# A mixture-of-experts layer: GpSimd's computing behind the routing moved to VectorE and ScalarE

## The chip, the cores and the metric

The kernel runs on one core of a Trainium2 chip (trn2). The metric is the device time of one execution in microseconds, as the median of several runs. The engines are named as in the profile: PE is TensorE's matmuls, PEld its weight loads, DVE is VectorE, ACT is ScalarE, POOL is GpSimd, SP is SyncE, whose queue issues most transfers. Matmuls run at one of two clock levels, 1.2 or 2.4 GHz; the profile gives the granted clock as a share of the higher.

## What is computed

One transformer layer on 512 tokens of width 2048, in float32: a projection, three mixers (spatial gating, a chunked recurrence, latent attention), an output projection, a layer norm, a router that picks two of 32 experts for each token, the experts, and a last layer norm. The change touches what comes behind the router:

```python
def hierarchical_moe(x, ...):
    # group_prob, top 1 group; in it the top 2 experts; gates = g_val * softmax(e_val)
    ...
    def run_block(args):
        xb, e = args
        h = jax.nn.silu(xb @ w_gate[e]) * (xb @ w_up[e])
        return h @ w_down[e]
    ys = lax.map(run_block, (xs, blk_exp)).reshape(P, D)
    out = jnp.zeros((N + 1, D), x.dtype).at[slot_tok].add(ys * slot_gate[:, None])
    return out[:N].reshape(B, S, D)
...
ffn = hierarchical_moe(x, ...)
x = layer_norm(DEEPNORM_ALPHA * x + ffn, ln2_g, ln2_b)
```

## The kernel before, in words

The program is written out by hand for each engine: every engine runs its instructions in the order in which the Python code issues them, and waits on semaphores where one needs another's result. Tokens lie in four blocks of 128 (`NB`), the width in 16 pieces of 128 (`KD`). `z[b]` holds a block's residual, later its result.

**Weights.** `Ring` streams weight chunks of 128x1024 float32 (512 KB) in the order of use. SP loads a chunk into a raw buffer (line 81); ACT copies its high part in float32r (line 96), DVE subtracts to get the low part (line 97), into one of four pairs of buffers (three in `whl`, one in an X slot). PE multiplies by both parts. `done` gives a pair back and `pump` issues the next copy, subtraction and load. The second and fourth quarter of each down projection (`WHOLE`) use the raw chunk as it is, without a split.

**Experts.** For each of the 32 experts `gather` zeroes one of two row buffers (`xgs`, slots M0 and B3, 128x2048; line 1202 for the first two, line 1328 for the others) and fetches the tokens' rows by an indirect transfer of POOL (line 1323), so many as the expert has, in eight sizes. `rows` turns them on PE (1348), applies ln1's gain on ACT and DVE (1437, 1364) and splits them (161, 162). `up` runs 16 chunks: four matmuls each (1390, 1391) if the expert has at most 64 rows, six (156 to 158) if more. `down` of the expert before runs behind it: four quarters of two chunks, each evicted with the gate as scale on ACT (1430), then `scatter` adds the rows to `yd` in DRAM by indirect transfers of POOL (1338). In the loop, pass e begins with `gather(e + 2)`, then comes `up(e)`, with the row work of expert e + 1 hooked between the chunks, then `down(e - 1)`. Behind pass 12 and pass 29 SP loads a layer norm's gain and bias, broadcast to 128 partitions (line 1554).

**Gates.** `gates` (1282 to 1296) turns the tokens' gates into a table by expert: a product and a subtraction on POOL (1283, 1287), a copy on ACT between them (1286), eight matmuls (1291), two steps on DVE. It is hooked into `up(0)`, the matmuls stand ahead of its last chunk.

**Tail.** Behind the last scatter the halves of `yd` are loaded back in 512 KB pieces (line 1578, `H` is the two halves of the width, `yd[i]` half i of all tokens), seven by SP and one by POOL. Each block is then: addition to `z` with the sum taken along (`add`, 1629), mean, squares on ACT (1638), root on ACT (1591, 1592) with a refinement on DVE (1597 to 1605), and the normalization in two passes (`norm`, 1610; `scale_dve`, 1617) with a store for each piece. POOL and ACT take block 3's additions (1632, 1635) and the normalization of block 1 and a quarter of block 3 (1622, 1626).

## Time and profile before

| | us |
|---|---|
| median of 3 runs | 1947.78 |
| lowest, highest | 1945.18, 1947.96 |
| the profiled execution, its own time | 1946.49 |
| span of its trace | 1944.7 |
| busy in it: PE, DVE, ACT, POOL | 1818.7, 1422.1, 1260.5, 277.1 |

The span runs from the first to the last instruction of the trace, 1.8 us under the time of the same execution. Times in the rows count from the span's start. The routing ends near 760, the experts run from there to about 1890, the tail follows. An engine's busy time is an average over all of these, so each is read by itself. In the rows "idle before" is how long the engine stood still ahead of the row, and behind the arrow is what ended that wait; the releaser is inferred. A row of the windows view gives a stretch and its length, then busy time and count of PE, PEld, DVE, ACT and POOL, the granted clock, the DMA share and GB/s.

### The profile page before, as it was taken

To read this page: it belongs to the slowest core of one execution; us is meant where nothing else is said; L and a number is where in the kernel's file an instruction comes from. 1 tells how busy PE (TensorE), PEld (TensorE's weight loads), DVE (VectorE), ACT (ScalarE), POOL (GpSimd) and SP (SyncE) were. 2 spreads that over 40 slices of the span, in tenths; PEclk is the share of its full clock that TensorE was granted. 3 is DMA by queue.
4 is the path that set the end of the run, shared out by engine and by line. 5 is a ranking of instruction groups with operands and counts; after the bars stand their busy time and mean duration, and the time that the engine had idled before them with its cause. 6 is when DMAs were issued, how large, how long until landed. Compare 5 with 4: busy or idle time off the path is not lost.

```text
span 1944.7 us, 25279 instructions
## 1 busy us (share of the span) xinstructions
PE 1818.7 (94%) x8235; PEld 1370.1 (70%) x8236; DVE 1422.1 (73%) x2031; ACT 1260.5 (65%) x1763; POOL 277.1 (14%) x200
## 2 busy tenths in 40 slices
PE   9999999999999996899999999999999999999980
PEld 7888888887787895666666666666766666667640
DVE  5656433566564456888989888898898989898757
ACT  4533363635452224788878888887888878788753
POOL 1000000020000001212121121212112121121114
PEclk9999999999999997899999999999999999999995
DMA  7222223223154225799999999999999999999983
GB/s 250 97 87 76 76 76 98 87 87 130 44 209 155 91 83 202 264 361 383 388 385 384 389 337 399 396 379 390 375 373 398 389 382 389 381 372 391 331 284 137
DMA packets 139942, 510.72 MB, mean 263 GB/s; under 512 B 17664, under 2 KB 17712, under 8 KB 137200
## 3 DMA queue, kind: packets, MB, share of 16 engines
q1 hardware_dynamic: 130608, 476.64, 65.2%
q0 software_dynamic: 8576, 30.26, 6.0%
q8 instruction: 93, 1.52, 0.3%
q10 hardware_dynamic: 576, 1.57, 0.2%
q14 instruction: 89, 0.73, 0.1%
HBM read 488.53 MB, written 22.02 MB: 263 GB/s over the span
## 4 chain that ended last, share of the span: by engine, by line
issue 50%; PE 36%; POOL 6%; DVE 4%; DMA 2%; POOLq 1%; ACT 0%; another core or an unknown queue 0%; SPq 0%; ACTq 0%; DVEq 0%
PE acc L156 10%; PE acc L157 10%; PE acc L158 10%; POOL yd L1338 2%; POOL B L1328 2%; POOL M L1328 1%; DMA yd<-M,idx 1%; POOLq L1309 1%; PE aux L495 1%; PE acc L860 1%; DMA B<-x1d,idx 1%; DVE B L1617 0%; PE acc L861 0%; POOLq L1315 0%; PE aux L831 0%
## 5 line engine op out<-in xcount | busy, mean ns | idle before, releaser
L97 DVE TENSOR_TENSOR whl<-X,whl 128x1024 fp32r<-128x1024 f32 x312 | 377.4, 1221 | 100.0 <-ACT whl L96 68.5
L97 DVE TENSOR_TENSOR whl<-wraw,whl 128x1024 fp32r<-128x1024 f32 (+1 forms) x222 | 269.6, 1217 | 227.6 <-ACT whl L96 210.1
L96 ACT ACTIVATE whl<-wraw 128x1024 fp32r<-128x1024 f32 (+1 forms) x222 | 235.2, 1063 | 220.7 <-PE acc L157 94.7
L96 ACT ACTIVATE whl<-X 128x1024 fp32r<-128x1024 f32 x312 | 330.8, 1074 | 60.9 <-PE acc L158 40.3
L1391 PE MATMUL acc<-whl,B 128*128 128x512 f32 x696 | 288.2, 414 | 15.6 <-DVE whl L97 15.6
L1390 PE MATMUL acc<-whl,B 128*128 128x512 f32 x696 | 295.0, 424 | 1.4 <-ACT whl L96 0.7
L1338 POOL DMA_INDIRECT yd<-M,idx x64 | 89.5, 1399 | 870.3 <-ACT M L1430 870.3
L1391 PEld LDWEIGHTS acc<-whl,B 128*128 128x128 f32 x696 | 132.0, 190 | 86.8 <-DVE whl L97 59.5
L158 PE MATMUL acc<-whl,B 128*128 128x512 f32 (+1 forms) x480 | 181.3, 378 | 0.0
L157 PE MATMUL acc<-whl,B 128*128 128x512 f32 (+1 forms) x424 | 166.0, 391 | 14.6 <-DVE whl L97 14.5
L156 PE MATMUL acc<-whl,B 128*128 128x512 f32 (+1 forms) x424 | 179.2, 423 | 0.0
L1390 PEld LDWEIGHTS acc<-whl,B 128*128 128x128 f32 x696 | 132.0, 190 | 31.8 <-issue 4.3
L156 PE MATMUL acc<-X,whl 128*128 128x512 f32 x384 | 151.1, 394 | 0.1
L157 PE MATMUL acc<-X,whl 128*128 128x512 f32 x384 | 149.7, 390 | 0.2 <-DVE X L162 0.2
L158 PE MATMUL acc<-X,whl 128*128 128x512 f32 x384 | 149.6, 390 | 0.0
L1426 PE MATMUL acc<-X,X 128*128 128x512 f32 x308 | 141.2, 592 | 0.0
L97 DVE TENSOR_TENSOR X<-X,X 128x1024 fp32r<-128x1024 f32 x105 | 128.0, 1219 | 17.5 <-ACT X L96 13.2
L96 ACT ACTIVATE X<-X 128x1024 fp32r<-128x1024 f32 x105 | 112.6, 1073 | 20.4 <-PE acc L158 15.0
L1430 ACT ACTIVATE M<-acc,X 128x512 f32<-128x512 f32 x128 | 87.4, 683 | 50.8 <-PE acc L1426 44.2
L157 PEld LDWEIGHTS acc<-whl,B 128*128 128x128 f32 x424 | 80.5, 190 | 47.7 <-DVE whl L97 27.0
L1391 PE MATMUL acc<-X,B 128*128 128x512 f32 x232 | 98.0, 422 | 9.4 <-DVE X L97 9.4
L158 PEld LDWEIGHTS acc<-whl,B 128*128 128x128 f32 x480 | 91.0, 190 | 15.7
(461 smaller groups left out, 3660.4 us busy)
## 6 DMA issues: line engine op xcount, KB each, us to landing
X<-w_down SPq DMA_DIRECT2D x169, 512.0 KB
X<-w_gate SPq DMA_DIRECT2D x160, 512.0 KB
X<-w_up SPq DMA_DIRECT2D x160, 512.0 KB
wraw<-w_gate SPq DMA_DIRECT2D x69, 512.0 KB
wraw<-w_up SPq DMA_DIRECT2D x69, 512.0 KB
wraw<-w_in SPq DMA_DIRECT2D x64, 512.0 KB
wraw<-w_down SPq DMA_DIRECT2D x64, 512.0 KB
B<-w_up SPq DMA_DIRECT2D x27, 512.0 KB
```

Of the source, the lines that this page charges most:

```text
L96: nc.scalar.activation(h[:, s], r[:, s], AF.Copy)
L97: nc.vector.tensor_tensor(l[:, s], r[:, s], h[:, s].bitcast(F32), op=OP.subtract)
L156: mm(o, a[0], b[0], start=start, stop=False)
L157: mm(o, a[0], b[1], start=False, stop=False)
L158: mm(o, a[1], b[0], start=False, stop=stop)
L495: mm(ov[r, j], fl(D)[:, c * P:c * P + r.stop], Dv[:, c, :, 1, :], start=True, stop=True)
L1328: nc.gpsimd.memset(xgs[e % 2], 0.0)
L1338: nc.gpsimd.indirect_dma_start(out=yd[i][:], out_offset=off(index), in_=y[:, H[i]], in_offset=None, bounds_check=T - 1, oob_is_err=False, ...
L1390: mm(o, x, wk[0], start=k == 0, stop=False)
L1391: mm(o, x, wk[1], start=False, stop=k == KD - 1)
L1426: mm(o, hfs[e % 2][:, k * P:(k + 1) * P], w[:, cs], start=k == 0, stop=k == 3)
L1430: act(yts[-1][:, n * 512:(n + 1) * 512], o, AF.Copy, scale=gt[:, EX[e]:EX[e] + 1])
```

## The change

Nothing but indirect transfers stays on POOL behind the routing. (1) `clear` zeroes a row buffer on ACT, as a copy of the constant `one_c`, broadcast over 2048 columns, with scale 0. It replaces the memsets; the first two stand behind `exps`, where the memsets stood ahead of the last block's routing. (2) The product and the subtraction of `gates` go to DVE. (3) The loads of the tail all go through SP, first half of all blocks first. (4) The tail's additions, normalizations and refinements run on DVE, block by block; ACT keeps the squares and the root; `add_pool`, `total`, `norm_act` and `gain` are gone. The last block's second pass goes in four quarters, the others' in halves.

```diff
--- before.py
+++ after.py
@@ -1198,8 +1198,9 @@
     ring.add([r1[:, 0, :]], once=True)
     ring.pump()
     xgs = [slot(t, [DM]) for t in ("M0", "B3")]
-    for t in xgs:
-        nc.gpsimd.memset(t, 0.0)
+
+    def clear(t):
+        act(t, one_c.to_broadcast([P, DM]), AF.Copy, scale=0.0)
 
 
     SIZES = (16, 24, 32, 40, 48, 64, 80, P)
@@ -1257,6 +1258,8 @@
 
     weave(rt_, ranks())
     exps()
+    for t in xgs:
+        clear(t)
     tt(oa[:, L], oh4[:, 0, L], oh4[:, 1, L], op=OP.add)
     mm(o3[:, 0:NE], afterr, oa[:, L], start=False, stop=True)
     mm(oc[:, 0:NE], onesr, oa[:, L], start=False, stop=True)
@@ -1280,11 +1283,11 @@
     gt = carve(NE)
 
     def gates():
-        nc.gpsimd.tensor_tensor(gv, oh, wide(gate, [2 * NB, NE], 2), op=OP.mult)
+        tt(gv, oh, wide(gate, [2 * NB, NE], 2), op=OP.mult)
         hl = tp[:, 0:512].rearrange("p (i a e) -> p i a e", a=2, e=NE)
         yield
         act(hl[:, :, 0], gv, AF.Copy)
-        nc.gpsimd.tensor_tensor(hl[:, :, 1], gv, hl[:, :, 0].bitcast(F32), op=OP.subtract)
+        tt(hl[:, :, 1], gv, hl[:, :, 0].bitcast(F32), op=OP.subtract)
         yield
         o = aux()
         for i in range(2 * NB):
@@ -1325,7 +1328,7 @@
                                          bounds_check=T - 1, oob_is_err=False)
         if e:
             if e > 1:
-                nc.gpsimd.memset(xgs[e % 2], 0.0)
+                clear(xgs[e % 2])
             sized(e, move)
         else:
 
@@ -1573,9 +1576,9 @@
 
     Q = [slice(i * 512, (i + 1) * 512) for i in range(4)]
     ys = [[slot(t, [DM]) for t in ts] for ts in (("M0", "B3"), ("B4", "X1"), ("B7", "X2"), ("X6", "X3"))]
-
-    for i, b in ((0, 0), (0, 1), (0, 2), (1, 0), (1, 1), (0, 3), (1, 2), (1, 3)):
-        (nc.gpsimd if (i, b) == (0, 2) else nc.sync).dma_start(ys[b][1][:, H[i]], yd[i][b * P:(b + 1) * P])
+    for i in range(2):
+        for b in range(NB):
+            nc.sync.dma_start(ys[b][1][:, H[i]], yd[i][b * P:(b + 1) * P])
     sums = carve(NB, 12)
     nc.scalar.preload_act_table_set("natural_log_exp_and_others")
 
@@ -1609,91 +1612,46 @@
         for s in parts:
             stt(ys[b][1][:, s], z[b][:, s], col(b, 8), lng2[:, s], op0=OP.add, op1=OP.mult)
 
-    def store(b, s):
-        nc.sync.dma_start(out[b][:, s], z[b][:, s])
-
-    def scale_dve(b, parts):
+    def scale(b, parts=H):
         for s in parts:
             stt(z[b][:, s], ys[b][1][:, s], rs[:, b:b + 1], lnb2[:, s], op0=OP.mult, op1=OP.add)
-            store(b, s)
-
-    def norm_act(b, parts):
-        for s in parts:
-            act(z[b][:, s], z[b][:, s], AF.Identity, scale=rs[:, b:b + 1], bias=col(b, 7))
-
-    def gain(b, s):
-        for t, op in zip((lng2, lnb2), (OP.mult, OP.add)):
-            nc.gpsimd.tensor_tensor(z[b][:, s], z[b][:, s], t[:, s], op=op)
-
-    def add(b, s, i):
+            nc.sync.dma_start(out[b][:, s], z[b][:, s])
+
+    def add(b, i):
+        s = H[i]
         stt(z[b][:, s], z[b][:, s], 1.0, ys[b][1][:, s], op0=OP.mult, op1=OP.add, accum_out=col(b, i))
 
-    def add_pool(b, s):
-        nc.gpsimd.tensor_tensor(z[b][:, s], z[b][:, s], ys[b][1][:, s], op=OP.add)
-
-    def total(b, s, i):
-        act(ys[b][0][:, s], z[b][:, s], AF.Copy, accum_out=col(b, i))
-
-    def squares(b):
+    def stats(b):
+        add(b, 1)
+        ts(col(b, 8), col(b, 0), col(b, 1), -1.0 / DM, op0=OP.add, op1=OP.mult)
         act(ys[b][0], z[b], AF.Square, bias=col(b, 8), accum_out=col(b, 9))
 
-    def run(*seq):
-
-        for f in seq:
-            if callable(f):
-                f()
-            else:
-                next(f, None)
-
-    for b in range(3):
-        add(b, H[0], 0)
-    add(0, H[1], 1)
-    mean(0)
-    squares(0)
-    root(0)
+        r = rs[:, b:b + 1]
+        act(r, col(b, 9), AF.Ln, scale=1.0 / DM, bias=eps2_c)
+        act(r, r, AF.Exp, scale=-0.5)
+
+    def refine(b):
+
+        r, v, t = rs[:, b:b + 1], col(b, 10), col(b, 11)
+        ts(v, col(b, 9), 1.0 / DM, EPS2, op0=OP.mult, op1=OP.add)
+        stt(t, r, v, r, op0=OP.mult, op1=OP.mult)
+        ts(t, t, -0.5, 1.5, op0=OP.mult, op1=OP.add)
+        tt(r, r, t, op=OP.mult)
+
+    for b in range(NB):
+        add(b, 0)
+    stats(0)
     norm(0, H[:1])
-    add(1, H[1], 1)
-    mean(1)
-    squares(1)
-    root(1)
-    add_pool(3, H[0])
-    total(3, H[0], 0)
-    add_pool(3, H[1])
-    f = refine(0)
-    run(f, lambda: norm(0, H[1:]), f, f, f)
-    scale_dve(0, H[:1])
-    for _ in refine(1):
-        pass
-    norm_act(1, H[:1])
-    gain(1, H[0])
-    add(2, H[1], 1)
-    mean(2)
-    squares(2)
-    root(2)
-    total(3, H[1], 1)
-    norm_act(1, H[1:])
-    gain(1, H[1])
-    scale_dve(0, H[1:])
-    norm(2, H[:1])
-    f = refine(2)
-    run(f, f, f, f)
-    scale_dve(2, H[:1])
-    mean(3)
-    squares(3)
-    root(3)
-    store(1, H[0])
-    norm(2, H[1:])
-    scale_dve(2, H[1:])
-    norm(3, H[:1])
-    f = refine(3)
-    run(f, f, f, f, f)
-    scale_dve(3, H[:1])
-    store(1, H[1])
-    norm_act(3, Q[3:])
-    gain(3, Q[3])
-    norm(3, Q[2:3])
-    scale_dve(3, Q[2:3])
-    store(3, Q[3])
+    stats(1)
+    norm(0, H[1:])
+    stats(2)
+    refine(0)
+    scale(0)
+    stats(3)
+    for b in range(1, NB):
+        norm(b)
+        refine(b)
+        scale(b, Q if b == NB - 1 else H)
 
 
 # ---- launch: one core; the host only lays the inputs out
```

Lines of the new kernel lie three higher from `clear` on: 1430 there is 1433, 1437 is 1440.

On ACT, where one expert's down projection ends and the next pass begins: the eviction of the fourth quarter, then the weight copy of the new pass and the gain step on the rows. Before:

```order
L1430 ACTIVATE M_118_6828<-acc,X_101_3986 128x512
L1315 UNCONDITIONAL_BRANCH
L1384 UNCONDITIONAL_BRANCH
L96 ACTIVATE whl<-wraw 128x1024
L1315 UNCONDITIONAL_BRANCH
L1437 ACTIVATE B_109_5391<-aux,X_101_3986 128x128
```

And now:

```order
L1433 ACTIVATE M_118_6828<-acc,X_101_3986 128x512
L1203 ACTIVATE M_108_5390<-one_c 128x2048
L1318 UNCONDITIONAL_BRANCH
L1387 UNCONDITIONAL_BRANCH
L96 ACTIVATE whl<-wraw 128x1024
L1318 UNCONDITIONAL_BRANCH
L1387 UNCONDITIONAL_BRANCH
L1440 ACTIVATE B_109_5391<-aux,X_101_3986 128x128 x2
```

The clear of a row buffer (`M_108`, slot M0; the next one takes `B_109`, slot B3) stands between the eviction and the copy that follows it.

On DVE in `up(0)`, around the last chunks, weight splits (97) and row splits (162). Before, the gates' steps stood on POOL and not here:

```order
L162 TENSOR_TENSOR B_115_6113<-B_109_5391,B_115_6113 128x512
L97 TENSOR_TENSOR whl<-X_105_5381,whl 128x1024
L1384 UNCONDITIONAL_BRANCH
L97 TENSOR_TENSOR whl<-X_105_5381,whl 128x1024
L162 TENSOR_TENSOR B_115_6113<-B_109_5391,B_115_6113 128x512
L1384 UNCONDITIONAL_BRANCH
L97 TENSOR_TENSOR whl<-B_106_5382,whl 128x1024
L97 TENSOR_TENSOR X_96_3981<-M_107_5383,X_96_3981 128x1024
```

And now:

```order
L162 TENSOR_TENSOR B_115_6113<-B_109_5391,B_115_6113 128x512
L97 TENSOR_TENSOR whl<-X_105_5381,whl 128x1024
L1387 UNCONDITIONAL_BRANCH
L97 TENSOR_TENSOR whl<-X_105_5381,whl 128x1024
L1387 UNCONDITIONAL_BRANCH
L162 TENSOR_TENSOR B_115_6113<-B_109_5391,B_115_6113 128x512
L97 TENSOR_TENSOR whl<-B_106_5382,whl 128x1024
L1290 TENSOR_TENSOR X_110_5395<-X_101_3986,X_110_5395 128x8x32
L97 TENSOR_TENSOR X_96_3981<-M_107_5383,X_96_3981 128x1024
```

The gates' subtraction (1290), which waits for ACT's copy, now has its place between two weight splits.

On SP, the loads of the tail; `yd_2918` and `yd_2919` are the two halves of the sums, and B_125, X_127, X_129, X_131 are blocks 0 to 3. Before:

```order
L1578 DMA B_125_20168<-yd_2918 128x1024
L1578 DMA X_127_20170<-yd_2918 128x1024
L1315 UNCONDITIONAL_BRANCH
L1578 DMA B_125_20168<-yd_2919 128x1024
L1578 DMA X_127_20170<-yd_2919 128x1024
L1578 DMA X_131_20174<-yd_2918 128x1024
L1578 DMA X_129_20172<-yd_2919 128x1024
L1578 DMA X_131_20174<-yd_2919 128x1024
```

And now:

```order
L1581 DMA B_125_20168<-yd_2918 128x1024
L1581 DMA X_127_20170<-yd_2918 128x1024
L1318 UNCONDITIONAL_BRANCH
L1581 DMA X_129_20172<-yd_2918 128x1024
L1581 DMA X_131_20174<-yd_2918 128x1024
L1581 DMA B_125_20168<-yd_2919 128x1024
L1581 DMA X_127_20170<-yd_2919 128x1024
L1581 DMA X_129_20172<-yd_2919 128x1024
L1581 DMA X_131_20174<-yd_2919 128x1024
```

Block 2's first half comes from POOL's queue to this one, and it and block 3's stand ahead of all second halves.

## Rows read from the trace of the kernel before

**Rows 1.** windows view: busy us (count) of five engines, PEclk, DMA, GB/s

```profile
1087.00:1105.00 18.00, 17.11 (x78) 12.08 (x76) 18.00 (x23) 18.00 (x27) 3.49 (x3) 1.00 1.03 384
```

**Rows 2.** timeline of ACT: start, us, line, operation, [idle before <-releaser]

```profile
1078.96 0.63 ACT L161 ACTIVATE B<-X 128x512 fp32r<-128x512 f32 x1 [2.99 <-DVE X L1407]
...
1084.83 0.69 ACT L1430 ACTIVATE M<-acc,X 128x512 f32<-128x512 f32 x1 [1.80 <-PE acc L1426]
...
1085.80 1.06 ACT L96 ACTIVATE whl<-wraw 128x1024 fp32r<-128x1024 f32 x1 [0.28 <-PE acc L1391]
```

**Rows 3.** timeline of DVE at the same change, first weight split

```profile
1086.89 1.22 DVE L97 TENSOR_TENSOR whl<-wraw,whl 128x1024 fp32r<-128x1024 f32 x1 [2.34 <-issue]
```

**Rows 4.** timeline of PE, last chunks of one expert, first of the next

```profile
1071.50 0.51 PE L157 MATMUL acc<-whl,B 128*128 128x512 f32 x1 [0.53 <-DVE whl L97]
...
1085.33 0.39 PE L1391 MATMUL acc<-whl,B 128*128 128x512 f32 x1
```

**Rows 5.** timeline of POOL over the experts: clears, one scatter

```profile
848.28 2.32 POOL L1328 MEMSET M<- 128x2048 f32 x1
...
1222.89 2.29 POOL L1328 MEMSET B<- 128x2048 f32 x1
...
1257.02 2.33 POOL L1328 MEMSET M<- 128x2048 f32 x1
...
1359.30 2.32 POOL L1328 MEMSET B<- 128x2048 f32 x1
...
1397.47 2.34 POOL L1328 MEMSET M<- 128x2048 f32 x1
...
1772.13 2.29 POOL L1328 MEMSET B<- 128x2048 f32 x1
...
1809.59 1.38 POOL L1338 DMA_INDIRECT yd<-M,idx  x1 [4.76 <-ACT M L1430]
```

**Rows 6.** timeline of SP at the first of two added loads

```profile
1212.07 0.42 SPq L1554 DMA_DIRECT2D X<-ln_g  x1
```

**Rows 7.** DMA view: issue, count, KB each of one added load

```profile
X<-ln_g SPq DMA_DIRECT2D x1, 1024.0 KB
```

**Rows 8.** timeline of POOL, PE and ACT in the first two experts

```profile
784.07 1.81 POOL L1328 MEMSET M<- 128x2048 f32 x1 [19.47 <-DVE B L162]
...
797.28 4.85 POOL L1287 TENSOR_TENSOR X<-X,X 128x256 fp32r<-128x256 f32 x1 [7.52 <-ACT X L1286]
...
766.74 2.79 PE L1348 MATMUL aux<-identr,M 128*128 128x128 f32 x12 [7.41 <-DMA M<-x1d,idx]
...
802.18 1.92 PE L1291 MATMUL aux<-X 128*128 128x64 f32 x8 [5.36 <-POOL X L1287]
...
782.73 1.06 ACT L96 ACTIVATE whl<-X 128x1024 fp32r<-128x1024 f32 x1 [0.57 <-PE acc L1391]
```

**Rows 9.** timeline of SP and POOL, loads ahead of the tail

```profile
1887.57 0.33 SPq L1578 DMA_DIRECT2D B<-yd  x1
...
1893.61 0.32 SPq L1578 DMA_DIRECT2D B<-yd  x1
...
1891.32 1.09 POOL L1578 DMA_DIRECT2D X<-yd  x1
```

**Rows 10.** timeline of DVE and ACT in the tail

```profile
1891.02 1.23 DVE L1629 SCALAR_TENSOR_TENSOR B<-B,B 128x1024 f32<-128x1024 f32 x1 [11.77 <-DMA B<-yd]
...
1899.20 1.22 DVE L1629 SCALAR_TENSOR_TENSOR B<-B,B 128x1024 f32<-128x1024 f32 x1 [2.18 <-DMA B<-yd]
...
1900.72 1.28 DVE L1610 SCALAR_TENSOR_TENSOR B<-B,X,X 128x1024 f32<-128x1024 f32 x1
...
1901.92 3.40 DVE L1629 SCALAR_TENSOR_TENSOR B<-B,X 128x1024 f32<-128x1024 f32 x1
...
1932.98 1.63 DVE L1617 SCALAR_TENSOR_TENSOR B<-X,X,B 128x512 f32<-128x512 f32 x1
...
1900.77 2.00 ACT L1638 ACTIVATE M<-B,X 128x2048 f32<-128x2048 f32 x1 [9.30 <-DVE X L1586]
```

## Prediction

> **What bounds the kernel now.** I read the kernel by stretches, since the change touches four of them: the end of the routing, the first two experts, the 28 experts in the steady loop, and the tail. In the loop GpSimd is nearly idle, so what matters is not what leaves GpSimd but what arrives on ScalarE, VectorE and the queues there.
>
> The clears of the loop mark its period: in the timeline of POOL they start at 848.28, 1222.89, 1257.02, 1359.30 and so on [rows 5]. From 848.28 to 1359.30 are 15 periods of 34.07 us; from 1397.47 to 1772.13 are 11 of 34.06. Two periods are longer: 1359.30 to 1397.47 (38.2), and the last one, which I read at the scatter at 1809.59.
>
> One period is a closed loop through three engines, read from who waits for whom. After the last matmul of an expert's first weight chunk (PE, 1085.33 to 1085.72 [rows 4]) ScalarE starts the copy that refills the pair of buffers this chunk freed, at 1085.80 [rows 2], and the row names PE as the releaser. VectorE takes the low part at 1086.89, after 2.34 idle [rows 3]. From there VectorE is never idle: 18.00 of 18.00 us busy from 1087 to 1105, and ScalarE, which feeds it, as full [rows 1]. PE keeps waiting for it (0.53 at 1071.50, one period earlier [rows 4]) until the last down-projection chunks, and from there PE runs unbroken to the next expert's first chunk, 1071.50 to 1085.72. So VectorE's run, about 14 us of PE and one short hop over ScalarE add up to 34.06. Anything put into that hop lengthens the period.
>
> The transfers look as full as VectorE (DMA share 1.03 in the same window [rows 1]), and would be the other candidate for the bound. What speaks against them: at 1212 the kernel loads two extra tensors, of 1024 KB [rows 6, 7], about 5 us of traffic at 384 GB/s, and the periods around it are 34.1 (1222.89 to 1257.02) like all others [rows 5].
>
> **Part 1, clears in the loop.** Each POOL memset of 128x2048 (2.3 us [rows 5]) goes, and one ScalarE copy of 128x2048 comes, right behind the eviction of the last down-projection quarter and ahead of the copy at 1085.80, as the order of ScalarE shows. ScalarE has no such instruction in the trace. A copy of 128x512 lasts 0.63, one of 128x1024 1.06 [rows 2], so 128x2048 lasts about 1.06 + 2 x 0.42 = 1.90; the Square of that shape lasts 2.00 [rows 10]. Neighbours overlap by about 0.1 (eviction at 1084.83 with 0.69, next possible start about 1085.41), so the clear holds ScalarE 1.79. It would start at 1085.41 and let the copy go at 1087.20 instead of 1085.80: **+1.40 us in the hop**. It waits for nothing else: the last reader of the buffer, the row split on VectorE, is done before the down projection. Queued behind it are the weight copies, the two gain steps on the rows, and through them VectorE and PE. ScalarE's own idle ahead of 1085.80 (0.28 in the row) is what it can hide in, and that is already counted. The bounds of one: 1.75 held (+1.36) and 2.00 with no overlap (+1.61).
>
> (The Trainium skill, "ScalarE: Activation LUTs", section "What ACT_TABLE_LOAD costs", gives an activation with immediate scale and bias 186 ns plus 0.833 ns per element, less some 93 ns overlap: an estimate of 1.80 held, and +36.7 us in all by the count below, where the rows give 36.4; no row of before has the operation itself.)
>
> There are 28 such clears. In the two long periods the expert has more than 64 rows, takes six matmuls for each chunk instead of four, and PE sets the pace; there the clear hides. 26 x 1.40 = **+36.4** (35.4 to 41.9). What POOL's memset gives back by leaving: nothing. The memset of that expert starts near 848.28 + 7 x 34.07 = 1086.8, so VectorE's split at 1086.89 runs beside it, and at 1.23 it is as short as an addition of that shape in the tail before POOL computes (1.23 at 1891.02 [rows 10]). The gather that follows starts no later, and its rows are needed one period later.
>
> **Part 2, the first two experts and the gates.** The two clears after the routing hold ScalarE some 3.6 us ahead of three weight copies; PE then stands for 7.41 until the first gathered rows arrive at 766.74 [rows 8], and wants the copies only after those rows are turned and split: nothing. The clear for the third expert waited 19.47 on POOL for VectorE until 784.07, now ScalarE waits there, with its copy of 782.73 behind it [rows 8]: that goes at about 784.0 + 1.8 = 785.8, 3.1 late, and VectorE after it by as much. Against this, PE waited 5.36 for POOL's gate subtraction of 4.85 us (797.28 to 802.13) before 802.18 [rows 8]. On VectorE it costs at most a 128x1024 pass of 1.23 [rows 3]. But it stands there behind the splits, which the clear has made some 3 late, so it ends at about 801 to 801.5: 0.5 to 1 gained, up to 3 if part of the delay is caught up. The fourth clear waits for VectorE in the same way, in an expert that PE paces: 0 to 2 lost. Sum **0** (-3 to +3).
>
> **Part 3, the tail.** Two things. First, the loads: yd's half for block 2 came through POOL at 1891.32, behind the last scatter; now it and block 3's go on SP right behind the first at 1887.57. The load of the second half, at 1893.61, took until 1899.20, 5.6 us, the first one 3.45 (1887.57 to 1891.02) [rows 9, 10]; the difference is the POOL load in its way. Without it 1897.4: 1.8 gained; none if the earlier loads hold up the scatter instead, and 1 lost if they do so by more.
>
> Second, VectorE from there to its end (1899.20 to 1932.98 + 1.63 = 1934.61, 35.4 us). It has passes of 1.2 that last 3.40 (1901.92, where POOL adds at the same time), and a last half pass of 1.63 [rows 10]. These stretches go; the work that POOL and ScalarE did comes to VectorE. Counted anew by undisturbed spacings (addition and mean 1.52, 1899.20 to 1900.72; a pass 1.20, 1900.72 to 1901.92; small steps 0.25, by the 0.3 of that mean): 4 x 1.52 + 14 x 1.20 (8 norms, 6 scales) + 4 quarter scales x 0.65 + 4 x 4 x 0.25 = 6.1 + 16.8 + 2.6 + 4.0 = 29.5. So 5.9 gained. ScalarE's squares (2.00 [rows 10]) end before VectorE asks for them. After its end both kernels have a 256 KB store to finish. Sum 5.9 + 1.8 = **-7.7** (-4.9 to -9.5, the latter with small steps of 0.15).
>
> **Sum.** 36.4 + 0 - 7.7 = +28.7. On the profiled 1946.49: 1975.2; that execution lies 1.3 under the median, so **1976**. By the bounds: 35.4 - 3 - 9.5 = +22.9 to 41.9 + 3 - 4.9 = +40.0, which is 1971 to 1988.
>
> **Rivals.** (a) *The transfers set the period.* Then the 1.40 is absorbed, since ScalarE only waits less for data, and the rest remains: 1947.8 - 7.7 = 1940, faster. For it: the share of 1.03. Against it: the extra loads that cost nothing, and a releaser on PE at the decisive copy. It decides if the 13.1 MB of a period (384 GB/s x 34.06) can't come faster than they do. (b) *The loop gives some back.* VectorE stands idle for 2.34 and more in each period [rows 3]; if work that is now behind the run can move up into that stretch, so that half of 1.40 vanishes, the loop costs 18 and the time is 1947.8 + 18 - 7.7 = 1958. Against it: VectorE takes its work in a fixed order, and its run has no gap to shorten [rows 1]. (c) *PE's clock.* The granted clock is 1.00 in the loop [rows 1]. VectorE's later start puts up to 1.4 more waiting on PE early in each expert; if the clock fell from 2.4 to 1.2 GHz there, matmuls would last twice as long, and PE, which is 95% busy (17.11 of 18.00 [rows 1]), would lose by estimate some 4 us in each period: 26 x 4 on top, about 2080. (The Trainium skill, "TensorE: Matmul & The Clock Gate", Part 1, says that the clock follows how busy PE has been; by that rule a thinner loop is at risk; the trace has no loop as thin.) Against it: PE already waits in the loop (0.53 at 1071.50 [rows 4]) and the clock holds.
>
> **How the numbers follow.** Forecast 0.80, (a) 0.08, (b) 0.09, (c) 0.03. The range reaches over the forecast's bounds and (b): 1957 to 1988. About 0.2% (3.9 us) is what a measurement of this kernel can tell from no change. Faster is (a): 0.08; the same, a mix of (a) and (b), 0.03; slower 0.89.
>
> **What would show it.** The starts of the indirect gathers should lie 35.4 to 35.5 apart, two of them 38.2; VectorE's idle ahead of its first split in each expert should grow from 2.34 to about 3.7, with the same 18 us run behind. In the tail no pass of 1024 columns on VectorE should last over 1.3, and its end should come about 36 us after the first addition, where it was 43.6 (1891.02 to 1934.61). The prediction is wrong if the gathers stay 34.06 apart, or if ScalarE's clear is much off 1.9.

## The result

The changed kernel takes 1973.42 us (median of 4 runs, 1972.23 to 1981.21) where the kernel before takes 1947.72: 25.7 us more. The ratio of the two is 1.0145, with a 95% interval of 1.013 to 1.016. The forecast was 1976, in a range of 1957 to 1988. The profiled execution took 1972.23, with a span of 1970.3, 25.6 over the span of before, and this difference can be split by landmarks that both traces have. The landmarks are the starts of POOL's indirect transfers, VectorE's first addition and its end in the tail.

| us | before | after | difference | forecast |
|---|---|---|---|---|
| start to the scatter of the first expert (its second half) | 847.37 | 848.50 | +1.13 | 0 |
| 28 experts of the loop, to the scatter of expert 28 | 962.22 | 998.34 | +36.12 | +36.4 |
| from there to the last scatter | 80.85 | 82.17 | +1.32 | 0 |
| last scatter to VectorE's first addition | 0.58 | 0.61 | 0 | 0 |
| first addition to the first of the second half | 8.18 | 7.67 | -0.5 | -1.8 |
| from there to VectorE's end | 35.41 | 28.75 | -6.7 | -5.9 |
| VectorE's end to the end of the span | 10.09 | 4.26 | -5.8 | 0 |

Four views of the changed kernel's loop answer to [rows 1 to 4]. The windows view of 18 us behind VectorE's first split of an expert (columns as in [rows 1]):

```profile
1064.50:1082.50 18.00, 16.58 (x72) 11.36 (x72) 18.00 (x24) 18.00 (x26) 0.00 (x0) 1.00 1.02 367
```

The timelines of ACT, DVE and PE at the same change of expert:

```profile
1060.13 0.69 ACT L1433 ACTIVATE M<-acc,X 128x512 f32<-128x512 f32 x1 [1.80 <-PE acc L1429]
1060.72 1.90 ACT L1203 ACTIVATE M<-one_c 128x2048 f32<-128x2048 f32 x1
1062.52 1.04 ACT L96 ACTIVATE whl<-B 128x1024 fp32r<-128x1024 f32 x1
```

```profile
1063.60 1.23 DVE L97 TENSOR_TENSOR whl<-B,whl 128x1024 fp32r<-128x1024 f32 x1 [3.75 <-ACT whl L96]
```

```profile
1060.63 0.39 PE L1394 MATMUL acc<-whl,B 128*128 128x512 f32 x1
```

The row of PE is the last of the four matmuls of the first chunk, as in [rows 4]. It is done at 1061.02, but the copy that this releases starts at 1062.52, 1.50 later instead of 0.08 (1085.72 to 1085.80), since the clear (1.90, start to next start 1.80) stands between it and the eviction. VectorE's idle time grows from 2.34 [rows 3] to 3.75, its releaser is now the copy, and behind it VectorE is busy for 18.00 of 18.00 as before. The DMA share reads 1.02 at 367 GB/s, where [rows 1] has 1.03 at 384.

POOL's timeline in the changed kernel: gathers, which now mark the period, and the scatters that bound the table's stages.

```profile
848.50 1.39 POOL L1341 DMA_INDIRECT yd<-M,idx  x1 [4.73 <-ACT M L1433]
850.29 1.01 POOL L1326 DMA_INDIRECT M<-x1d,idx  x1 [0.40 <-ACT M L1203]
...
1382.02 0.97 POOL L1326 DMA_INDIRECT B<-x1d,idx  x1 [0.43 <-ACT B L1203]
...
1420.41 0.95 POOL L1326 DMA_INDIRECT M<-x1d,idx  x1 [0.52 <-ACT M L1203]
...
1810.29 0.96 POOL L1326 DMA_INDIRECT B<-x1d,idx  x1 [0.46 <-ACT B L1203]
...
1846.84 1.37 POOL L1341 DMA_INDIRECT yd<-M,idx  x1 [4.78 <-ACT M L1433]
...
1929.01 1.32 POOL L1341 DMA_INDIRECT yd<-M,idx  x1 [4.85 <-ACT M L1433]
```

From 850.29 to 1382.02 are 15 periods of 35.45, from 1420.41 to 1810.29 are 11 of 35.44; the one between them is 38.39. Against [rows 5] that is +1.39 in each of 26 periods, and nothing in the two that PE paces (38.32 and 38.35 from scatter to scatter, 38.33 and 38.34 before).

The tail on DVE (timeline), which answers to [rows 10]:

```profile
1929.62 1.22 DVE L1622 SCALAR_TENSOR_TENSOR B<-B,B 128x1024 f32<-128x1024 f32 x1 [11.89 <-DMA B<-yd]
...
1937.29 1.23 DVE L1622 SCALAR_TENSOR_TENSOR B<-B,B 128x1024 f32<-128x1024 f32 x1 [2.23 <-DMA B<-yd]
...
1940.01 1.22 DVE L1622 SCALAR_TENSOR_TENSOR B<-B,X 128x1024 f32<-128x1024 f32 x1
...
1963.30 2.74 DVE L1617 SCALAR_TENSOR_TENSOR B<-X,X,B 128x512 f32<-128x512 f32 x4
```

The addition that lasted 3.40 beside POOL [rows 10] now lasts 1.22, and VectorE ends at 1966.04. What follows differs most. In before, POOL computed almost as long as VectorE (its last row on the timeline of POOL):

```profile
1932.47 1.59 POOL L1626 TENSOR_TENSOR B<-B,B 128x512 f32<-128x512 f32 x1
```

The windows view of the last stretches of before, then of after (last columns: clock, DMA share, GB/s):

```profile
1936.00:1937.00 1.00, 0.00 (x0) 0.00 (x0) 0.00 (x0) 0.00 (x0) 0.00 (x0) 0.50 0.94 322
1937.00:1938.00 1.00, 0.00 (x0) 0.00 (x0) 0.00 (x0) 0.00 (x0) 0.00 (x0) 0.50 0.02 2
1938.00:1944.70 6.70, 0.00 (x0) 0.00 (x0) 0.00 (x0) 0.00 (x0) 0.00 (x0) 0.50 0.00 0
```

```profile
1967.00:1968.00 1.00, 0.00 (x0) 0.00 (x0) 0.00 (x0) 0.00 (x0) 0.00 (x0) 0.50 0.90 305
1968.00:1969.00 1.00, 0.00 (x0) 0.00 (x0) 0.00 (x0) 0.00 (x0) 0.00 (x0) 0.50 0.07 27
1969.00:1970.30 1.30, 0.00 (x0) 0.00 (x0) 0.00 (x0) 0.00 (x0) 0.00 (x0) 0.50 0.00 0
```

Before, no engine and no transfer does anything for the last 6.7 us; after, that is less than 2.

### The profile page after: what moved, and what is told of

It is laid out like the page before. It is cut to its first block, busy times and chain, and to the rows that moved or that the text cites. A ratio compares the mean times of both kernels' runs of the same rounds, so it can differ in the third digit from the quotient of the medians.

```text
span 1970.3 us, 25238 instructions
## 1 busy us (share of the span) xinstructions
PE 1834.7 (93%) x8235; PEld 1370.8 (70%) x8236; DVE 1413.5 (72%) x2041; ACT 1307.5 (66%) x1788; POOL 157.2 (8%) x157
## 4 chain that ended last, share of the span: by engine, by line
issue 50%; DMA 6%; DVE 2%; POOL 1%; POOLq 1%; ACT 0%; PE 0%; DVEq 0%; ACTq 0%
DMA yd<-M,idx 5%; POOL yd L1341 1%; DVE B L1617 0%; POOLq L1312 0%; DVE X L1613 0%; DVE whl L97 0%; DVE B L1622 0%; DMA X<-w_up 0%; POOLq L1318 0%; ACT whl L96 0%; DMA B<-w_down 0%; DMA B<-yd 0%; POOLq L1341 0%; DVE B L1613 0%; DVE X L97 0%
## 5 line engine op out<-in xcount | busy, mean ns | idle before, releaser
L157 PEld LDWEIGHTS acc<-whl,B 128*128 128x128 f32 x424 | 80.5, 190 | 47.6 <-DVE whl L97 27.0
```

Source lines behind the costliest of these rows:

```text
L157: mm(o, a[0], b[1], start=False, stop=False)
```

## The experiments

The table gives each run's stages as above: S the scatter of the first expert, L the 28 experts of the loop, R from there to the last scatter, T from the last scatter to the end of the span, and E the part of T behind VectorE's end. They are read from the profiled execution. The times are medians, those of half_clear, loads_alone, pool_at_end, gates_alone and first_clears of one execution; the kernel before took 1945.8 to 1946.2 in these comparisons.

| | time | S | L | R | T | E |
|---|---|---|---|---|---|---|
| before | 1947.7 | 847.4 | 962.2 | 80.9 | 54.3 | 10.1 |
| after | 1973.4 | 848.5 | 998.3 | 82.2 | 41.3 | 4.3 |
| clears_alone | 1990.8 | 853.9 | 998.3 | 80.4 | 53.7 | 10.1 |
| pool_clears | 1931.0 | 843.0 | 962.1 | 80.8 | 42.2 | 4.3 |
| clear_earlier | 1943.3 | 850.9 | 967.4 | 80.7 | 42.2 | 4.3 |
| clear_in_idle | 1936.5 | 852.1 | 961.9 | 81.1 | 42.3 | 4.2 |
| half_clear | 1944.2 | 844.0 | 976.3 | 80.4 | 41.7 | 4.3 |
| tail_alone | 1935.4 | 848.0 | 961.8 | 82.7 | 41.8 | 4.2 |
| loads_alone | 1946.1 | 847.4 | 962.0 | 82.8 | 52.2 | 10.0 |
| last_quarter | 1939.7 | 846.3 | 962.0 | 81.8 | 47.6 | 4.1 |
| pool_at_end | 1942.0 | 848.8 | 962.0 | 82.6 | 46.9 | 8.7 |
| gates_alone | 1943.1 | 843.9 | 962.4 | 81.6 | 53.4 | 10.1 |
| first_clears | 1945.0 | 846.3 | 962.3 | 80.9 | 53.8 | 10.1 |
| idle_pool23 | 1930.3 | 842.8 | 962.1 | 81.9 | 42.3 | 4.2 |

### The clears in the loop

**clears_alone**: before, with only this line changed (and `clear` defined).

```
-                nc.gpsimd.memset(xgs[e % 2], 0.0)
+                clear(xgs[e % 2])
```

> The kernel before, with only the 30 clears of gather(2) to gather(31) moved from POOL to ACT, in the place that the change gives them; first clears, gates and tail stay as before. Theory (the clear stands in the hop between PE's first chunk and DVE's first split): 26 periods of 35.45 instead of 34.06 (+36.1), +1.3 in the last pass as in the changed kernel, and up to +3 in the second expert, where ACT's copy for the gates now runs late and POOL's subtraction of 4.85 still follows it: 1985 to 1988. Rival (the clears hide and the 26 us come from another part of the change): within 3 us of 1947.7.

Measured: 1990.77, ratio 1.0234 (1.021 to 1.0258), L = 998.34, the same as in the changed kernel. The whole of the loop's loss is this one line. The early part lost 6.5 us, more than the 3 expected: PE's wait for POOL's subtraction is still there, and now comes later (timeline of PE; 802.18 with 5.36 in [rows 8]).

```profile
806.33 1.91 PE L1294 MATMUL aux<-X 128*128 128x64 f32 x8 [5.37 <-POOL X L1290]
```

**pool_clears**: the changed kernel with that line as before, the opposite edit.

```
-                clear(xgs[e % 2])
+                nc.gpsimd.memset(xgs[e % 2], 0.0)
```

> The changed kernel, with only the 30 clears of gather(2) to gather(31) back on POOL; first clears on ACT, gates on DVE and the new tail stay. Theory: periods of 34.06 again, so 1973.4 - 36.1 - 1.3 = 1936, and 1 to 3 less where the third expert's clear no longer holds up ACT: 1933 to 1936. Rival (part of the tail's 13 us hangs on POOL computing nothing at all behind the routing, not on what it does in the tail): the last store's end lies 7 to 8 us ahead of the span's end again, and the time is 1939 to 1942.

Measured: 1930.95, ratio 0.9929 (0.9912 to 0.9946), L = 962.10, E = 4.27. All else in the change is, taken together, a gain, and this kernel beats both of the others. It came out below the expected 1933, since the clears for the third and fourth expert weigh more than I took (below).

**clear_earlier**: the same number of clears on ACT, moved ahead by one eviction.

```
-            if e > 1:
+            if e in (2, 3):
                 clear(xgs[e % 2])
...
+            if n == 2 and e + 4 < NE:
+                clear(xgs[e % 2])
```

> The changed kernel with the clears of gather(4) to gather(31) on ACT as well, but one weight copy earlier: behind the copy that follows the third eviction of the down projection, ahead of the fourth eviction, where ACT stands idle for 1.80 us in each expert. The same instructions on the same engine. Theory (only the hop counts): the clear of 1.79 fits into the idle time, the periods are 34.06 to 34.2, and the time is 1973.4 - 36.1 - 1.3 = 1936, up to 1940. Rival (ACT is full, so 1.8 us more on it cost 1.4 wherever they stand): periods of 35.4, 1970 to 1975.

Measured: 1943.31, ratio 0.9992 (0.9982 to 1.0002). The idea that ACT's total work sets the pace falls: 28 clears on ACT, and 31 of the 36 us are gone. But not all, and the time lies over the expected 1940. The first eleven periods are 34.02 to 34.09; later, where VectorE also applies a layer norm, they are 34.45 to 34.50, two of them 34.9. ACT's timeline in an early and in a late expert:

```profile
1052.35 1.90 ACT L1203 ACTIVATE M<-one_c 128x2048 f32<-128x2048 f32 x1
1054.26 0.69 ACT L1433 ACTIVATE M<-acc,X 128x512 f32<-128x512 f32 x1
1055.23 1.06 ACT L96 ACTIVATE whl<-B 128x1024 fp32r<-128x1024 f32 x1 [0.28 <-PE acc L1394]
...
1502.31 1.91 ACT L1203 ACTIVATE B<-one_c 128x2048 f32<-128x2048 f32 x1
1504.11 0.68 ACT L1433 ACTIVATE M<-acc,X 128x512 f32<-128x512 f32 x1
1504.68 1.06 ACT L96 ACTIVATE whl<-X 128x1024 fp32r<-128x1024 f32 x1
```

In the early expert the copy waits for PE again, by the same 0.28 as in [rows 2]; in the late one it follows the eviction without a wait, so the clear has pushed both. The idle time of that place is smaller there, as ACT's timeline of pool_clears shows at the same point:

```profile
1488.91 0.63 ACT L161 ACTIVATE B<-X 128x512 fp32r<-128x512 f32 x1 [4.28 <-DVE X L1410]
...
1493.49 0.69 ACT L1433 ACTIVATE M<-acc,X 128x512 f32<-128x512 f32 x1 [0.90 <-PE acc L1429]
```

0.90 ahead of the fourth eviction instead of 1.80, and 4.28 three instructions earlier, where VectorE applies the layer norm's gain and bias.

**clear_in_idle**: the clear goes there.

```
-            if n == 2 and e + 4 < NE:
+            if n == 0 and e + 4 < NE:
```

> As clear_earlier, but the 28 clears stand behind the weight copy that follows the first eviction of the down projection. There ACT waits 2.99 us for VectorE's fold of the partial sums in the first experts and 4.3 us from expert 13 on, where VectorE also applies a layer norm's gain and bias; ahead of the fourth eviction it waits 1.80 in the first and only 0.90 in the others. Theory (a clear costs what it exceeds the idle time of its place by, as far as the first split of the next expert waits for it): clear_earlier had periods of 34.05 up to expert 12 and of 34.47 from 13 on; here all normal periods are 34.05, and the time is 1943.3 less 14 x 0.42 = 1937. Rival (the 0.42 come from ACT's total work in the richer periods): they stay at 34.47, 1943.

Measured: 1936.49, ratio 0.995 (0.9936 to 0.9965), L = 961.91, all normal periods 34.01 to 34.09. ACT's timeline shows what is left of the idle time in an early and a late expert:

```profile
1046.65 1.91 ACT L1203 ACTIVATE M<-one_c 128x2048 f32<-128x2048 f32 x1
1049.51 0.63 ACT L161 ACTIVATE B<-X 128x512 fp32r<-128x512 f32 x1 [0.96 <-DVE X L1410]
...
1493.54 1.91 ACT L1203 ACTIVATE B<-one_c 128x2048 f32<-128x2048 f32 x1
1497.73 0.63 ACT L161 ACTIVATE B<-X 128x512 fp32r<-128x512 f32 x1 [2.29 <-DVE X L1410]
```

0.96 and 2.29: a clear of 1.9 costs nothing here. The same instruction costs 36 us, 5 us or nothing by its place alone.

**half_clear**: the clear of the hop, cut in two.

```
-                clear(xgs[e % 2])
+                act(xgs[e % 2][:, H[0]], one_c.to_broadcast([P, DM // 2]), AF.Copy, scale=0.0)
+                nc.gpsimd.memset(xgs[e % 2][:, H[1]], 0.0)
```

> The changed kernel with each of the 30 clears of gather(2) to gather(31) cut in two: 1024 columns on ACT in the hop, the other 1024 on POOL. Theory (the hop takes what exceeds the 0.39 of slack there): a 128x1024 copy holds ACT for 0.95, so periods of 34.06 + 0.56 = 34.6 and 1952. Rival (the cost goes by the work on ACT): half of 1.39, periods of 34.75, 1955. Rival (POOL's memset beside DVE's first splits costs too): over 34.8.

Measured: normal periods of 34.56 to 34.65, mean about 34.60. That is the theory's 34.6 and not 34.75, so the hop absorbs a fixed part of what is put into it and passes on the rest. POOL's half beside VectorE's splits costs nothing. The time (1944.2) lies under the expected 1952 mostly because the early part gained 4.5 us, which I had not counted.

### The first two experts

**gates_alone**: before, with the two steps of `gates` on VectorE.

```
-        nc.gpsimd.tensor_tensor(gv, oh, wide(gate, [2 * NB, NE], 2), op=OP.mult)
+        tt(gv, oh, wide(gate, [2 * NB, NE], 2), op=OP.mult)
...
-        nc.gpsimd.tensor_tensor(hl[:, :, 1], gv, hl[:, :, 0].bitcast(F32), op=OP.subtract)
+        tt(hl[:, :, 1], gv, hl[:, :, 0].bitcast(F32), op=OP.subtract)
```

> The kernel before, with only the gates' product and subtraction on VectorE. Theory (PE's wait for the subtraction was POOL's 4.85 us): PE's wait ahead of the gates' matmuls falls from 5.36 to some 2.2, the value of the changed kernel, and the scatter of the first expert's second half comes at 844 to 845 instead of 846.3 to 848.0 (four executions with before's code up to there); time about 3 less, 1943 to 1945. Rival (the subtraction waits behind the splits on VectorE as long as POOL took): the scatter stays at 847.

Measured: S = 843.9, about 3.5 earlier (2.4 to 4.1 against the four executions that the expectation names). PE's timeline, against 802.18 with 5.36 in [rows 8]:

```profile
798.62 1.92 PE L1291 MATMUL aux<-X 128*128 128x64 f32 x8 [2.25 <-DVE X L1287]
```

**first_clears**: before, with the two first clears on ACT behind the routing.

```
-    for t in xgs:
-        nc.gpsimd.memset(t, 0.0)
...
     exps()
+    for t in xgs:
+        clear(t)
```

> The kernel before, with only the two first clears moved from POOL, ahead of the last block's routing, to ACT, behind it. Theory (the memsets held up POOL's small steps of the routing, which the first gather waits for): the first gather starts at about 758.0 instead of 760.4, and 1 to 2 of these 2.4 us arrive at the first expert's scatter (845 to 846 instead of 847.3): 1944 to 1947. Rival (the clears hold up ACT's three weight copies by as much): gather earlier, scatter at 847 to 848.

Measured: the first gather at 758.26 instead of 760.42, S = 846.25, 1.1 earlier than in before. That the clears held up the first gather is shown; how much of the 2.2 arrives is not, since the four executions with before's code up to there lie at 846.3 to 848.0.

**idle_pool23**: clear_in_idle, with the clears for the third and fourth expert on POOL.

```
             if e in (2, 3):
-                clear(xgs[e % 2])
+                nc.gpsimd.memset(xgs[e % 2], 0.0)
```

> As clear_in_idle (28 clears on ACT behind the first eviction), but the clears for the third and fourth expert, which wait for VectorE among the first two experts' weight copies, are on POOL again. Theory (these two clears on ACT cost 5 to 8 us: 848.5 to 852.1 at the first expert's scatter in three executions, against 843.0 and 844.0 where POOL has them or half of them): scatter at 843 to 844, periods of 34.05, 1930 to 1932, the same as pool_clears. Rival (the early difference is chance of the executions): 1936, as clear_in_idle.

Measured: 1930.32, ratio 0.9912 (0.9893 to 0.9932), S = 842.8. So the two early clears on ACT cost 5 to 9 us: 9.3 between clear_in_idle and this kernel, 5.5 between the changed kernel and pool_clears, 6.5 between clears_alone and before, pairs whose code differs up to that scatter by these two clears alone. (pool_at_end has the clears on POOL as well and an S of 848.8, but its first gather came 6 us late; from the first gather to S it takes 84.4, pool_clears 85.2, the changed kernel 90.5.) PE's timelines show where it begins, first in the changed kernel, then in pool_clears:

```profile
787.14 0.44 PE L1351 MATMUL aux<-identr,B 128*128 128x128 f32 x2 [3.98 <-ACT B L1440]
```

```profile
783.33 0.44 PE L1351 MATMUL aux<-identr,B 128*128 128x128 f32 x2 [0.57 <-ACT B L1440]
```

DVE's timeline of the changed kernel has three waits there for ACT's copies, where pool_clears has none:

```profile
786.43 1.22 DVE L97 TENSOR_TENSOR whl<-X,whl 128x1024 fp32r<-128x1024 f32 x1 [2.92 <-ACT whl L96]
...
790.52 1.23 DVE L97 TENSOR_TENSOR whl<-X,whl 128x1024 fp32r<-128x1024 f32 x1 [0.45 <-ACT whl L96]
...
793.17 1.23 DVE L97 TENSOR_TENSOR whl<-B,whl 128x1024 fp32r<-128x1024 f32 x1 [0.79 <-ACT whl L96]
```

### The tail

**tail_alone**: before, with all of the new tail and nothing else.

```
-    for i, b in ((0, 0), (0, 1), (0, 2), (1, 0), (1, 1), (0, 3), (1, 2), (1, 3)):
...
+    for i in range(2):
+        for b in range(NB):
...
```

> The kernel before with only the new tail (loads and all that follows). Theory: the 13.0 us between the last scatter and the end in the changed kernel belong to the tail's code alone: 1934 to 1936. Rival (5.5 of them, between the last byte stored and the end of the span, come because POOL computes nothing behind the routing; here it still clears and computes the gates): 1939 to 1942.

Measured: 1935.38, ratio 0.9947 (0.9935 to 0.9959), T = 41.8 and E = 4.2. What POOL does before the tail (here it still clears and computes the gates) has no part in it.

**loads_alone**: before, with only the order and the queue of the loads changed, as in tail_alone's diff.

> The kernel before, with only the tail's loads changed: all eight on SP, first halves first. Theory (the loads are worth the 0.5 us between the first addition and that of the second half, and the 5.8 at the very end are POOL's): 8.18 between these additions becomes 7.7, DVE's end to the span's end stays at 10, 1945 to 1948. Rival (the load on POOL's queue is what the end waits for): 10.1 becomes 4.3, 1941 to 1942.

Measured: 1946.1, E = 10.0, and the stretch between the first addition and that of the second half did not shrink: 8.24. SP's timeline shows why:

```profile
1889.24 0.33 SPq L1579 DMA_DIRECT2D B<-yd  x1
1889.61 1.38 SPq L1579 DMA_DIRECT2D X<-yd  x3
1897.43 0.32 SPq L1579 DMA_DIRECT2D B<-yd  x1
```

The load of the second half goes 8.19 after that of the first, where it was 6.04 [rows 9]. It waits for the last scatter, and two more loads of 512 KB are now in that scatter's way: the DMA view has the scatter landing 5.3 after its issue at 1892.10, where in before the load that waits for it goes 3.17 after it, and in the us from 1892.50 on the DMA share is 1.03, where before has 0.50 and 0.58 in the two behind its scatter's issue. The load itself is quicker (3.3 to VectorE's addition at 1900.74, against 5.6), and the two cancel. T is 2.1 shorter all the same: POOL's first addition (1897.27) now falls into VectorE's wait and its second (1905.88) beside one small step, where before they stood beside two passes, which lasted 3.40 and 3.06.

**last_quarter**: before, with block 3's last quarter on VectorE.

```
-    norm_act(3, Q[3:])
-    gain(3, Q[3])
     norm(3, Q[2:3])
     scale_dve(3, Q[2:3])
-    store(3, Q[3])
+    norm(3, Q[3:])
+    scale_dve(3, Q[3:])
```

> The kernel before, with only the last quarter of block 3 on DVE, so that POOL's last computation lies some 10 us ahead of the end. Theory (the end waits for POOL where it has computed just before): DVE's end to the span's end falls from 10.1 to 4.3; DVE has two more passes of 512 columns (0.66 each), without POOL beside it its last ones fall from 1.7 to 0.66 each: 1941 to 1943. Rival (any computing of POOL in the tail costs that at the end): it stays at 10, and the time is 1946 to 1948.

Measured: 1939.67, ratio 0.9965 (0.995 to 0.998), a little under the expected 1941, E = 4.1. The timeline of POOL and the windows view of the end:

```profile
1921.41 2.34 POOL L1626 TENSOR_TENSOR B<-B,B 128x1024 f32<-128x1024 f32 x1
```

```profile
1935.00:1936.00 1.00, 0.00 (x0) 0.00 (x0) 0.00 (x0) 0.00 (x0) 0.00 (x0) 0.50 0.75 250
1936.00:1937.00 1.00, 0.00 (x0) 0.00 (x0) 0.00 (x0) 0.00 (x0) 0.00 (x0) 0.50 0.00 0
1937.00:1937.80 0.80, 0.00 (x0) 0.00 (x0) 0.00 (x0) 0.00 (x0) 0.00 (x0) 0.50 0.00 0
```

POOL adds beside VectorE in this tail as before, until 1923.75, and still the end follows the last bytes by 2 us. So it is only late computing that the end waits for.

**pool_at_end**: pool_clears with one tiny step on POOL, whose result nothing reads.

```
         refine(b)
+        if b == NB - 1:
+            nc.gpsimd.tensor_tensor(col(0, 7), rs[:, b:b + 1], rs[:, b:b + 1], op=OP.mult)
         scale(b, Q if b == NB - 1 else H)
```

> As pool_clears, with one tiny product of 128x1 on POOL added, behind the last block's refinement, some 2.7 us ahead of VectorE's end; its result is not used. In the kernel before POOL's last result lay 10.6 us ahead of the end of the span, and in last_quarter, with that result 14 us ahead, nothing was waited for. Theory (the end can't come sooner than some 10.6 us after POOL's last computation, whatever its size): DVE's end to the span's end grows from 4.27 to about 8, 1934 to 1936. Rival (only long POOL passes cost): it stays 4.3, 1931. Rival (a fixed price of 6 for computing on POOL late): 10.1, 1937.

Measured: E = 8.7, the theory's 8 and neither 4.3 nor 10.1. The time (1942.0) is higher than expected because this execution was already some 6 us late at the first gather (764.36, against 757.8 to 758.3 in the seven executions of other kernels with the changed first clears), where the edit can have no part. POOL's timeline, then the windows view:

```profile
1928.94 0.75 POOL L1655 TENSOR_TENSOR X<-X 128x1 f32<-128x1 f32 x1 [34.27 <-DVE X L1639]
```

```profile
1933.00:1934.00 1.00, 0.00 (x0) 0.00 (x0) 0.00 (x0) 0.00 (x0) 0.00 (x0) 0.50 0.53 178
1934.00:1940.30 6.30, 0.00 (x0) 0.00 (x0) 0.00 (x0) 0.00 (x0) 0.00 (x0) 0.50 0.00 0
```

POOL's step ends at 1929.69, and the span ends 10.61 later. In before, clears_alone, gates_alone, first_clears and loads_alone the span's end lies 10.57 to 10.67 behind the end of POOL's last addition.

## Why the prediction was right, and where it was not

**The loop: right, by its own steps.** The chain that the prediction named (PE's first chunk, one copy on ACT, VectorE's unbroken run) is the one that the clear lengthened. Its terms: the clear 1.90 forecast and 1.90 measured, held 1.79 and 1.80, per period 1.40 and 1.39, over 26 periods 36.4 and 36.1; the two PE-paced periods lost nothing. The Trainium skill's figure ("ScalarE: Activation LUTs", section "What ACT_TABLE_LOAD costs"), an estimate of 1.80 held, agrees with the trace. clears_alone and pool_clears show that it is the clears, clear_earlier and clear_in_idle that it is their place, half_clear that the hop had 0.39 us of room.

**The rivals.** That the transfers set the period (1940) falls: the periods grew by all of the hop's 1.39. The share that spoke for it, 1.03 in [rows 1], reads 1.02 in the changed kernel with 17 GB/s less, so it can't tell a full queue from a less full one. That the loop gives back half falls by the same number. PE's clock stayed at 1.00 (2.4 GHz) in each of the 28 stretches of 35.45 us from 850 to 1842.6, with PE busy for 16.58 of 18.00 in the window shown, so that rival falls too; its price of 4 us in each period follows from no row that it names. In the first two experts the granted clock is lower, 0.82 to 0.87 on the mean from the first gather to S in all fourteen executions, but it doesn't follow the clears: 0.86 in the changed kernel, 0.83 in the faster pool_clears.

**The first two experts: 0 forecast, +1.1 measured, within the bounds, but in part by luck.** The delay of VectorE's next split was right: 786.43 in the changed kernel against 783.19 in pool_clears, 3.2 for 3.1. What failed is that VectorE would be late "by as much" and no more: it waits again, 0.45 and 0.79, ahead of two later splits, and the gates' matmuls come 4.7 later (802.64 against 797.98 in pool_clears); with the fourth expert's clear it is 5.5 at S, and 5 to 9 over the three pairs, where the sum had 3 to 5. The gates' move was sized well: the subtraction takes 0.42 on VectorE and ends at 798.57 where no clear has delayed the splits, some 3 ahead of the 801 to 801.5 that the prediction had with the delay; it is worth about 3.5 alone, and in the changed kernel the clear takes all of it, not all but 0.5 to 1. And the step "the two clears after the routing: nothing" overlooked what POOL's memsets held up: they stood ahead of POOL's small steps of the last block's routing, and the first gather now goes 2.5 us earlier. The 5.5 lost and the 3.5 gained leave +2.0; what lies between that and +1.1 is of the size of the 1.1 that first_clears gained at S, but both are within the spread of the executions, so how much of the earlier gather arrives isn't shown. I had asked what the new clears would delay, and not what the old ones had.

**The stretch ahead of the last scatter: no effect shown.** +1.32 there is within what the fourteen executions show, 80.4 to 82.8 with no order by kernel. ACT waits for weights from DRAM in the last passes, and these waits vary: in the last but one, for chunks of `w_up`, 1.00 and 2.74 in the changed kernel, and none over 0.36 in before.

**The tail: -7.7 forecast, -13.0 measured.** VectorE's run was sized well (29.5 forecast, 28.75 measured: undisturbed passes of 1.22 to 1.28, small steps 0.13 to 0.26 apart). Beside POOL's addition of 2.33 from 1901.89 on, the addition of [rows 10] lasted 3.40, to 1.1 us behind POOL's end; beside POOL's memsets VectorE's splits leave the period at 34.06. Both agree with the Trainium skill ("SBUF — State Buffer", section "SBUF: two separate sides"), by which a VectorE operation with two inputs and a GpSimd operation that reads the memory take a shared pair of ports in turn, each for its whole instruction; a memset reads nothing.

The loads' term was wrong: -1.8 was taken, -0.5 came in the changed kernel, and that is the best of the nine executions with the new order, in which the stretch from the first addition to that of the second half takes 7.67 to 9.17; the five with the old order take 7.68 to 8.18. The alternatives that the prediction named (nothing gained, or 1 lost, because the earlier loads hold up the scatter) are what the runs show; in the changed kernel the last scatter lands 5.0 after its issue, and the stretch is shorter only by the quicker load behind it.

The step that failed is "After its end both kernels have a 256 KB store to finish". It is true of the store, which ends 2.3 to 2.4 after VectorE in both, and not of the end: before, the span went on for 7.7 us after the last byte, because POOL had computed until 1934.06. With these 5.8 the tail lies outside its own bounds (-4.9 to -9.5). I had read the timelines only up to VectorE's last row; the distance from there to the end of the span, 10.1 us, could be read from before alone and asked for a reason. That late computing on POOL is the reason is shown by last_quarter and pool_at_end; what POOL does in the 10.6 us no view shows, and it stays open.

Together: 1.13 + 36.12 + 1.32 - 12.97 = 25.6, where the forecast had 28.7. The range held the time because the loop's term, nearly three times any other, was right; of the tail's 5.3 too much, 2.4 were lost in the first experts and the last passes. Three slips in the working change nothing of this: [rows 3] has 1.22 where it reads 1.23, the loads' gain by its rows is 2.1 (1893.61 + 3.45 = 1897.06) and not 1.8, and the tail's -9.5 is -9.3 by its own terms (5.9 + 1.6 + 1.8).

**A better kernel.** pool_clears (1931.0) and idle_pool23 (1930.3) keep the new tail, the gates on VectorE and the first clears on ACT, and take the loop's clears out of the hop, to POOL or to ACT's idle time. By the medians of their comparisons they are 15 and 16 us under before (ratios 0.9929 and 0.9912), and not to be told from each other. The same with the old order of the loads was not run.

## What to carry to other kernels

Work that is moved to a busy engine is priced by what stands behind it in that engine's order, not by the engine's share: find the hop that closes the loop, and put the work into a wait that does not belong to it (0 instead of 36 us here, for the same instructions). A wait's length has to be read in every variant of the loop; 1.80 in the first experts was 0.90 in the later ones. And read the trace to the very end of the span: a gap in which nothing runs has a cause as well.

## What the runs showed that was not expected

Where GpSimd computed late, the span ended 10.57 to 10.67 us after its last computation, in six kernels, be that a 128x512 addition or a step of 128x1 that nothing reads. Computing on GpSimd that ends 14 us ahead of the end (last_quarter) costs nothing there. Whether an indirect transfer does the same no run shows: the changed kernel's last one, at 1929.01, lies 41 us ahead of its end.

VectorE's small steps pay for GpSimd as well as its long passes. In before, two of 128x1 lasted ten times as long as the others beside two passes of POOL (timelines of DVE and of POOL):

```profile
1917.45 2.05 DVE L1599 SCALAR_TENSOR_TENSOR X<-X 128x1 f32<-128x1 f32 x1
1919.54 0.15 DVE L1601 TENSOR_SCALAR X<-X 128x1 f32<-128x1 f32 x1
1919.73 2.07 DVE L1603 TENSOR_TENSOR X<-X 128x1 f32<-128x1 f32 x1
```

```profile
1916.28 3.20 POOL L1626 TENSOR_TENSOR B<-B,B 128x1024 f32<-128x1024 f32 x1
1919.45 2.33 POOL L1626 TENSOR_TENSOR B<-B,X 128x1024 f32<-128x1024 f32 x1
```

The two with two tensors as inputs ended with POOL's passes (1919.50 and 1921.80, against 1919.48 and 1921.78); the one with a single input between them didn't wait.
